# A hybrid decoder step: a quarter of the cached key pages split to fp16 rows in the even layer and transposed by DMA in the attention

## The chip, the cores and the metric

The kernel runs on one core of a Trainium2 chip. The metric is the device time of one launch in microseconds. Engine names are those of the profile: PE (TensorE matmuls), PEld (its weight loads), DVE (VectorE), ACT (ScalarE), POOL (GpSimd), SP (SyncE, whose queue issues most DMAs; its rows are named SPq).

## What is computed

One inference step of a decoder with two layers, for a prompt of 2048 tokens and for 8 sequences that each add 4 tokens to 2048 cached ones. The even layer has four heads of gated linear attention and four of "forgetting" attention, softmax attention with a bias from cumulated log forget gates; the odd layer is gated linear attention alone. The part that the change touches is the attention of the 8 sequences over their cached pages (a page is 128 tokens by 4 heads by 128 values, fp32; 16 pages a sequence, 128 in all, found through a page table):

```python
def fox_sample(q, k, v, log_f, k_pages, v_pages, logf_pages, page_table):
    k_past = k_pages[page_table].reshape(db, -1, H, dh)
    v_past = v_pages[page_table].reshape(db, -1, H, dh)
    ...
    logit_past = jnp.einsum('bthd,bshd->bhts', q, k_past).astype(jnp.float32) * scale \
        + cum_new[..., None] + suffix_past[:, :, None, :]
    ...
    p = jax.nn.softmax(jnp.concatenate([logit_past, logit_new], axis=-1), axis=-1).astype(v.dtype)
    return jnp.einsum('bhts,bshd->bthd', p[..., :P], v_past) + jnp.einsum('bhts,bshd->bthd', p[..., P:], v)
```

## The kernel before

Three phases follow each other on one core. `phase_even` computes the even layer's projections and its linear attention in two halves of 1024 tokens, `phase_fox` the forgetting attention of prompt and sequences, `phase_odd` both output projections, the odd layer and the final norm.

**Projections.** A product of fp32 values is made of three fp16 matmuls (`mm3`, L623 to L625: high times high, high times low, low times high). Weights are split into the two parts on the chip: ACT makes the high part (L353), DVE the low one (L354). A split needs a scale, a power of two, from the largest absolute value of the weights; for the weights of the output projections and of the odd layer it is measured early, beside the even layer's second half: `beside`, called from `staged`, runs `measure` (DVE's reductions at L300) and `scale` of the units in `later_units`. The names of their groups start with o (output projections), Cqk, Cv and Cg. A projection fills one of three PSUM banks (tag `pj`) and is copied out by ACT and DVE. The last unit is the attention's V (`Bv1`): DVE's copies and the low half at L1064 and L1071, ACT's high half at L1070, the stores to DRAM (`vd`) at L1085.

**Attention.** `fox_prompt` and `fox_sample` are generators; `until` draws from them in turn so that both advance by their shares FOX_P and FOX_S, and each `yield` tells what cost has been issued. A scheduler, which simulates the engines when the program is built, then puts the instructions of each engine in order; buffers are handed out by it when they come free. The prompt's blocks: scores (`s`, L623 to L625), bias and maximum on DVE (L1413), exponential with its sum on ACT (L1421), scaling on POOL (L1429), transposes on PE (L1449), split by ACT and DVE (L1456, L1457), and the product with V (`fo`). Its loads of q, k, v, bias and gate stand on SP's queue (L1375 to L1390), k by transposing DMA.

The sequences' keys go by 32 groups: 4 chunks of 512 tokens, in each the 8 sequences, for each 4 pages. A group's 4 pages are loaded by SP (L1543; the slots hold 25 pages). For each head, `turn` transposes its 4 pieces of 128 x 128 fp32 on PE into a PSUM bank (L1573, tag `kt`, two banks), and ACT (heads 0 and 2, L1577) or DVE (heads 1 and 3, L1578) copies them to one of eight key slots. Then `score` (L1632) multiplies the queries (32 columns for each head, zero but for this sequence's 4) with the 512 keys, as four fp32 strips side by side in the 32-column quarters of the array (`strips`). In the program a group's heads are turned before the group ahead of it is scored. After a chunk's 8 sequences, 16 small matmuls add the bias (L1661), and DVE takes the scores out with their running maximum (L1664). The values follow: 32 groups of 4 pages (L1711).

The sequences' queries (`qs`), keys, gates and values are loaded at L1555 and L1556, scaled by DVE (L1561), and spread to `qz` (L1565).

## Time and profile before

| | |
|---|---|
| median of 3 runs | 2329.38 us (2325.68 to 2329.55) |
| the profiled execution | 2327.94 us, span 2326.2 us |
| mean granted clock of TensorE | 0.991 |
| even layer's second half | about 480 to 856 us |
| attention, key pages | about 857 to 1077 us |
| attention, value pages | about 1077 to 1242 us |
| odd layer and output projections | from about 1272 us |

Times in the trace count from the span's start. A row of a timeline has the start, the length, the engine, line and operation, and in brackets the idle time of that engine just before and what ended it. The profiled execution is one more execution than the three of the median; it lies 0.06% below their median.

### The profile page before, as it was taken

To read this page: it belongs to the slowest core of one execution; us is meant where nothing else is said; L and a number is where in the kernel's file an instruction comes from. 1 tells how busy PE (TensorE), PEld (TensorE's weight loads), DVE (VectorE), ACT (ScalarE), POOL (GpSimd) and SP (SyncE) were. 2 spreads that over 40 slices of the span, in tenths; PEclk is the share of its full clock that TensorE was granted. 3 is DMA by queue.
4 is the path that set the end of the run, shared out by engine and by line. 5 is a ranking of instruction groups with operands and counts; after the bars stand their busy time and mean duration, and the time that the engine had idled before them with its cause. 6 is when DMAs were issued, how large, how long until landed. Compare 5 with 4: busy or idle time off the path is not lost.

```text
span 2326.2 us, 57896 instructions
## 1 busy us (share of the span) xinstructions
PE 2248.9 (97%) x23060; PEld 1604.3 (69%) x23060; DVE 1412.1 (61%) x3281; ACT 1018.5 (44%) x2264; POOL 733.7 (32%) x786
## 2 busy tenths in 40 slices
PE   7999999999999999999999999999999999999998
PEld 5667677855755875565446888677677666666887
DVE  7766568526654657667777445366675655557554
ACT  6434354211222225555566543545544544545343
POOL 2333334001201214223345345144552432322232
PEclk9999999999999999999999999999999999999999
DMA  7343444755432377875983969524234431115553
GB/s 238 120 128 105 146 127 164 201 142 160 143 120 73 125 189 251 245 242 196 276 262 102 335 195 263 132 79 137 74 102 96 121 96 58 49 56 164 176 181 150
DMA packets 357423, 361.64 MB, mean 155 GB/s; under 512 B 105777, under 2 KB 300658, under 8 KB 353058
## 3 DMA queue, kind: packets, MB, share of 16 engines
q1 hardware_dynamic: 355010, 351.33, 49.4%
q0 software_dynamic: 2144, 6.62, 0.8%
q8 instruction: 181, 2.97, 0.5%
q14 instruction: 88, 0.72, 0.1%
HBM read 244.54 MB, written 96.42 MB: 147 GB/s over the span
## 4 chain that ended last, share of the span: by engine, by line
PE 40%; DVE 5%; DMA 2%; ACT 2%; issue 1%; POOL 1%; SPq 1%; POOLq 0%; DVEq 0%; ACTq 0%
PE pt_o L623 4%; PE pt_o L624 4%; PE pt_o L625 4%; PE pt_Cv L623 2%; PE pt_Cv L624 2%; PE pt_Cv L625 2%; PE o_C L910 1%; PE gl_C L756 1%; PE pt L1449 1%; PE pv L1711 1%; DMA yr<-yT 1%; DMA wr_Cv<-in_w_in_odd 1%; PE py_C L728 1%; DVE scT L771 1%; PE fo L623 0%
## 5 line engine op out<-in xcount | busy, mean ns | idle before, releaser
L623 PE MATMUL pt_o<-w_o,act 128*128 128x256 f16 x1024 | 278.9, 273 | 1.9 <-ACT sg1C L680 1.9
L624 PE MATMUL pt_o<-w_o,act 128*128 128x256 f16 x1024 | 278.9, 273 | 0.0
L625 PE MATMUL pt_o<-w_o,act 128*128 128x256 f16 x1024 | 278.7, 273 | 0.0
L623 PEld LDWEIGHTS <-act 128*128 128x128 f16 x2304 | 226.1, 98 | 35.9 <-issue 3.6
L624 PEld LDWEIGHTS <-act 128*128 128x128 f16 x2304 | 226.2, 98 | 32.0 <-issue 3.4
L625 PEld LDWEIGHTS <-act 128*128 128x128 f16 x2304 | 226.2, 98 | 29.9 <-issue 1.7
L790 POOL TENSOR_TENSOR kA<-kA,fA 128x512 f32<-128x512 f32 (+1 forms) x56 | 80.9, 1445 | 344.8 <-PE gl_A L756 273.1
L623 PE MATMUL pt_Cv<-w_Cv,act 128*128 128x256 f16 (+1 forms) x512 | 141.3, 276 | 0.0
L624 PE MATMUL pt_Cv<-w_Cv,act 128*128 128x256 f16 (+1 forms) x512 | 141.3, 276 | 0.0
L625 PE MATMUL pt_Cv<-w_Cv,act 128*128 128x256 f16 (+1 forms) x512 | 141.2, 276 | 0.0
L790 POOL TENSOR_TENSOR kC<-kC,fC 128x512 f32<-128x512 f32 (+1 forms) x56 | 83.6, 1492 | 154.3 <-PE gl_C L756 103.1
L1429 POOL TENSOR_SCALAR L<-L,nm 128x512 f32<-128x512 f32 (+3 forms) x160 | 99.3, 635 | 103.5 <-DVE nm L1425 46.7
L1421 ACT ACTIVATE L<-L,nm,kc 128x512 f32<-128x512 f32 (+3 forms) x160 | 118.2, 740 | 27.5 <-DVE nm L1419 26.3
L1456 ACT ACTIVATE th<-pt 128x512 f16<-128x512 f32 (+3 forms) x159 | 81.8, 528 | 88.3 <-PE pt L1449 86.8
L1457 DVE TENSOR_TENSOR tl<-pt,th 128x512 f16<-128x512 f32 (+3 forms) x159 | 95.0, 609 | 20.7 <-ACT th L1456 18.9
L1449 PE MATMUL pt<-ident,L 128*128 128x128 f32 x544 | 91.4, 280 | 1.4 <-POOL L L1429 0.9
L1573 PEld LDWEIGHTS pkt<-ident,pgcache_fox_k 128*128 128x128 f32 x512 | 59.2, 142 | 44.2 <-issue 27.1
L1573 PE MATMUL pkt<-ident,pgcache_fox_k 128*128 128x128 f32 x512 | 78.5, 281 | 5.7 <-DVE kts L1578 1.7
L1449 PEld LDWEIGHTS pt<-ident,L 128*128 128x128 f32 x544 | 67.7, 144 | 23.3 <-DVE tl L1457 4.5
L1911 ACT ACTIVATE vC<-pt_Cv,kc 128x512 f32<-128x512 f32 (+1 forms) x40 | 23.9, 598 | 129.9 <-PE pt_Cv L625 129.9
L623 PE MATMUL pt_Bk<-w_Bk,act 128*128 128x256 f16 x256 | 70.2, 274 | 1.8 <-DVE Bvs L1071 1.8
L623 PE MATMUL pt_Av<-w_Ai,act 128*128 128x256 f16 x256 | 70.8, 277 | 0.5 <-ACT act L618 0.5
(959 smaller groups left out, 6566.6 us busy)
## 6 DMA issues: line engine op xcount, KB each, us to landing
pgcache_fox_k<-in_cache_fox_k SPq DMA_DIRECT2D x128, 256.0 KB, 4.2
pgcache_fox_v<-in_cache_fox_v SPq DMA_DIRECT2D x128, 256.0 KB, 4.2
yr<-yT SPq DMA_DIRECT2D x16, 1024.0 KB, 7.4
x1d<-xo SPq DMA_DIRECT2D x44, 256.0 KB, 4.7
wr_o<-in_w_out_even SPq DMA_DIRECT2D x32, 256.0 KB, 5.3
xo<-in_x_prompt SPq DMA_DIRECT2D x32, 256.0 KB, 5.5
wr_Cv<-in_w_in_odd SPq DMA_DIRECT2D x32, 256.0 KB, 3.9
x1r<-x1d SPq DMA_DIRECT2D x16, 512.0 KB, 4.9
```

Of the source, the lines that this page charges most:

```text
L623: nc.tensor.matmul(ps, lh[0], rh[0], start=first, stop=False)
L624: nc.tensor.matmul(ps, lh[0], rh[1], start=False, stop=False)
L625: return nc.tensor.matmul(ps, lh[1], rh[0], start=False, stop=last)
L728: nc.tensor.transpose(py[:, c * rows : (c + 1) * rows], on[:rows, c, t * P : (t + 1) * P], self.ident[:rows, :rows])
L790: nc.gpsimd.tensor_tensor(kv[:, :, 0], kv[:, :, 0], t1.to_broadcast([P, nb, w]), ALU.mult)
L1421: self.last_exp = nc.scalar.activation(lt[:, :w], lt[:, :w], AF.Exp, bias=nm[:, 0:1], scale=ib, accum_out=nm[:, 2 + j : 3 + j])
L1429: nc.gpsimd.tensor_scalar(lt[:, :w], lt[:, :w], nm[:, 1:2], 2.0**14, ALU.mult, ALU.mult)
L1449: nc.tensor.transpose(pt[:, w : w + P], rows[b][s // 4][0][:, (s % 4) * P : (s % 4 + 1) * P], self.ident)
L1456: nc.scalar.activation(th[:, a:w], pt[:, a:w], AF.Copy),
L1457: nc.vector.tensor_tensor(tl[:, a:w], pt[:, a:w], th[:, a:w], ALU.subtract)))
L1573: last = nc.tensor.transpose(pk[:, j * P : (j + 1) * P], pgs[j][:, h * P : (h + 1) * P], self.ident)
L1911: r = nc.scalar.activation(v[h][:, g : g + cnt], ps[:, :, :256], AF.Copy, scale=c)
```

## The change

Sequences 0 and 4 (`ROWED`), 32 of the 128 key pages, take another way.

In the even layer's second half, `page_rows` loads each of these pages, and for every row of a page (a token, all four heads) ACT adds up the absolute values, DVE bounds the sum from below and inverts it, ACT writes the scaled row as fp16 (the high part), DVE the remainder as fp16 (the low part), and SP stores 256 KB to DRAM (`kp`). `staged` draws from it at a pace (`PACE`): half a page at each step of 14 units and a whole one in the last. ACT's first step for a page also waits for the last projection matmul issued before it in the program. To make room on DVE, the measures named by `loose` (60 of those at L300) move to ACT, as sums of absolute values.

In the attention the 8 groups of these sequences come as two transposing DMAs of 512 KB each, straight into the layout that `score` needs: no transposes on PE, no copies. They are scored by 12 fp16 strips (`score3`: three products, four heads). As every row carries its own scale, `esc` brings the scales into the layout of the scores by 16 small matmuls a chunk, copied by ACT, and DVE's extraction multiplies by them instead of adding a zero; the bias is divided by the scales beforehand, and the other sequences' scales are 1. The queries are split to fp16 (`q16`, `qz16`).

Slots change: pages come in 6 slots of four, the turned keys have 4 slots instead of 8 (4 more, `pT`, serve the values' stage), the values' stage has 4 page slots of four. Group 0's two transposes and group 1's pages are asked for early, before the sequences' own loads.

```diff
+ROWED = (0, 4)
+SC_D = 10500.0
-S0 = 12000.0
+S0 = 6000.0
+SC_K = 1000.0
-FOX_S = 411000.0
+FOX_S = 500000.0
-PV_C = 5860.0
+PV_C = 5800.0
+PACE = [0] * 17 + [6] * 14 + [12]
...
+    def most(self, key, dst, x):
+        nc = self.nc
+        if not self.loose(key):
+            nc.vector.tensor_reduce(dst, x, mybir.AxisListType.XY, ALU.max, apply_absolute_value=True)
+            return
+        k, n = x.shape[1:]
+        nc.scalar.activation(self.junk()[:, : k * n].rearrange("p (k n) -> p k n", k=k), x, AF.Abs, scale=2.0**-10,
+                             accum_out=dst)
...
+        done = []
+        load(0)
+        for n in range(total):
+            load(n + 1)
+            m, s = self.km[:, n : n + 1], cols[n % 2]
+            x = fly.pop(n).rearrange("p (h d) -> p h d", h=NH)
+            t = pool.tile([P, NH, 2, P], F16, tag="pgs", name=f"kps{n}")
+            first = nc.scalar.activation(t[:, :, 0], x, AF.Abs, scale=2.0**-15, accum_out=m)
+            self.tc.add_manual_dep(first.ins, self.last_mm.ins.name, mybir.DependencyInfo(
+                mybir.DependencyClass.Sync, mybir.DependencyReason.DATA), reason="pages at the projections' pace")
+            nc.vector.tensor_scalar(m, m, TINY, None, ALU.max)
+            nc.vector.reciprocal(s, m)
+            nc.scalar.activation(t[:, :, 0], x, AF.Copy, scale=s)
+            nc.vector.scalar_tensor_tensor(t[:, :, 1], x, s, t[:, :, 0], ALU.mult, ALU.subtract)
+            if done:
+                store(*done.pop())
+            done.append((n, t))
+            yield
...
-                fs = Pool(s0, {"pg": PG, "kt": 8})
+                fs = Pool(s0, {"kt": 4, "pT": 4})
...
+        def page_cols(c, b):
...
+                for x in range(2):
+                    d = nc.sync.dma_start_transpose(
+                        t[:, 2 * x : 2 * x + 2].rearrange("p h x t -> p (h x) t"),
+                        self.kp[r : r + 512, x * 512 : (x + 1) * 512])
...
+            nc.vector.tensor_copy(q16[:, 0], qs)
+            nc.vector.tensor_tensor(q16[:, 1], qs, q16[:, 0], ALU.subtract)
+            for x in range(2):
+                for h in range(NH):
+                    nc.vector.tensor_tensor(qz16[:, x, h], q16[:, x, h : h + 1].to_broadcast([P, len(ROWED), TS]),
+                                            self.bmask[:, ROWED[0] :: ROWED[1] - ROWED[0]], ALU.mult)
...
+            if b in ROWED:
+                self.strips([score3(h, b, kt[0], sc, x, y) for x, y in ((0, 0), (0, 1), (1, 0)) for h in range(NH)],
+                            [kt[1]])
...
+                        nc.tensor.matmul(pe[32 * h : 32 * h + 32, j * P : (j + 1) * P],
+                                         env["sel"][:, 4 * c + j].rearrange("p b t -> p (b t)"), env["esc"][:, h],
+                                         start=True, stop=True, tile_position=(0, 32 * h))
+                et = fs.tile([P, 512], F32, tag="kt", name=f"escs{c}")
+                nc.scalar.activation(et, pe, AF.Copy)
```

How the instructions stand. The first place is SP's queue where the attention starts. Before, the last two loads of the prompt's second group, two stores of V (`vd`), the sequences' own loads, the last store of V, and the prompt's third group:

```order
L1386 DMA v_01_10717<-vd_74 128x4x256
L1390 DMA fsg_10722<-sgd 128x512
L1085 DMA vd_75<-Bvs_10537 128x2x512
L1085 DMA vd_75<-Bvs_10596 128x2x512
L1555 DMA qs<-qs 128x4x32
L1555 DMA kn<-ks 128x4x32
L1555 DMA sgs<-sgd 128x4x32
L1556 DMA vn<-vs 32x512
L1085 DMA vd_75<-Bvs_10655 128x2x512
L1382 DMA q_02_10793<-qd 128x2x512
```

Now, the same place up to the first page load (`kT` is a group of key pages as transposed by DMA; the last store of V is the one between the two):

```order
L1461 DMA_TRANSPOSE k_01_11419<-kd_72 128x2x512
L1452 DMA cb_11342<-cbd 128x512
L1617 DMA_TRANSPOSE kT_11356<-kp 128x4x512
L1108 DMA vd_75<-Bvs_11301 128x2x512
L1617 DMA_TRANSPOSE kT_11356<-kp 128x4x512
L1643 ISA
L1643 DMA pgcache_fox_k_11408<-in_cache_fox_k 128x512
```

and, after three more page loads like the last row, up to the sequences' first load:

```order
L1463 DMA v_01_11420<-vd_74 128x4x256
L1467 DMA fsg_11425<-sgd 128x512
L1459 DMA q_02_11496<-qd 128x2x512
L1461 DMA_TRANSPOSE k_02_11497<-kd_73 128x2x512
L1452 DMA cb_11342<-cbd 128x512
L1463 DMA v_02_11498<-vd_75 128x4x256
L1467 DMA fsg_11503<-sgd 128x512
L1672 DMA qs<-qs 128x4x32
```

The load of `qs` stood ahead of the last store of V; it now stands behind it, behind the second transpose, four page loads and two sets of the prompt's loads.

The second place is DVE at the same point, where the loaded queries are first read (`L` are the prompt's biased scores, `tl` low parts of its probabilities, `kts` turned keys). Before:

```order
L1457 TENSOR_TENSOR tl_10823<-pt_10819,th_10822 128x256
L1457 TENSOR_TENSOR tl_10856<-pt_10853,th_10855 128x128
L1419 TENSOR_SCALAR nm_10878<-mx_10864,kc 128x1
L1413 ISA L_10896,mx_10891<-s_10892,cb_10696 128x512
L1413 ISA mx_10891 128x1
L1413 ISA L_10902,mx_10891<-s_10898,cb_10696,mx_10891 128x384
L1413 ISA mx_10891 128x1
L1578 COPY kts_10992<-pkt_10987 128x512
L1413 ISA L_10902,mx_10891<-s_10898,cm_10889,mx_10891 128x128
L1413 ISA mx_10891 128x1
L1561 TENSOR_SCALAR qs<-qs,kc 128x64 x2
```

Now:

```order
L1490 ISA L_11596,mx_11591<-s_11592,cb_11342 128x512
L1490 ISA mx_11591 128x1
L1534 TENSOR_TENSOR tl_11526<-pt_11522,th_11525 128x256
L1676 CAST q_11367<-qs 128x128
L1703 COPY kts_11674<-pkt_11669 128x512
L1677 TENSOR_TENSOR q_11367<-qs,q_11367 128x128
L1680 TENSOR_TENSOR qz_11536<-q_11367,bmask 128x64 x4
L1685 TENSOR_SCALAR kn<-kn,kc 128x64 x2
```

The first reader of `qs`, the cast, stands ahead of the first copy of turned keys and of the scores that follow; before, the first reader stood behind both.

The third place is PE within a chunk, where a group's turning meets the scoring of the group ahead of it. Before:

```order
L1573 MATMUL pkt_12148<-ident,pgcache_fox_k_12146 128x128
L1632 MATMUL sc_12219<-kts_12026,qz 32x512
L1632 MATMUL sc_12219<-kts_12045,qz 32x512
L1632 MATMUL sc_12219<-kts_12052,qz 32x512
L1632 MATMUL sc_12219<-kts_12068,qz 32x512
L1573 MATMUL pkt_12162<-ident,pgcache_fox_k_12140 128x128
```

Now:

```order
L1698 MATMUL pkt_13263<-ident,pgcache_fox_k_13258 128x128 x4
L1769 MATMUL sc_12774<-kts_13157,qz 32x512
L1769 MATMUL sc_12774<-kts_13181,qz 32x512
L1769 MATMUL sc_12774<-kts_13188,qz 32x512
L1769 MATMUL sc_12774<-kts_13207,qz 32x512
L1698 MATMUL pkt_13282<-ident,pgcache_fox_k_13258 128x128 x4
L645 LDWEIGHTS v_03_11694
L645 MATMUL fo_13006<-th_13485,v_03_11694 128x128
```

The order is the same, the first head's transposes, the strips, the second head's transposes; but with four slots the copy of the first head's bank can only start behind the strips, and a prompt matmul follows ahead of the third head.

More of the change, by code (lines that the diff above doesn't have):

```diff
@@ L624, in mm3 @@
         nc.tensor.matmul(ps, lh[0], rh[1], start=False, stop=False)
-        return nc.tensor.matmul(ps, lh[1], rh[0], start=False, stop=last)
+        self.last_mm = nc.tensor.matmul(ps, lh[1], rh[0], start=False, stop=last)
+        return self.last_mm
     def proj_fm(self, pps, act, W, off, M, hf, evac, nm):
@@ L1141, in phase_even @@
             us, lins = [], []
+            self.pages = self.page_rows(wp)
+            self.paged = 0
+            self.junk = lambda: nrm.tile([P, D], BF16, tag="th", name="junk")
             def beside(x):
@@ L1290, in staged @@
                     beside(2 * j + n // 2)
+                if beside and j > 2:
+                    self.paged += PACE[j]
+                    while self.paged >= 12:
+                        self.paged -= 12
+                        next(self.pages, None)
                 yield c
@@ L1545, in page, with fetch @@
             return t, d
+        def fetch(n):
+            c, b = n // DB, n % DB
+            if b in ROWED:
+                return page_cols(c, b)
+            return [page("cache_fox_k", b, 4 * c + j)[0] for j in range(4)]
+        held, ahead = {}, {0: fetch(0)}
+        for nm, shape in (("vn", [TS, 512]), ("sgs", [P, NH, TS]), ("ys", [P, NH, DB, DS]), ("pTn", [TS, DB, NH, DS]),
+                          ("qs", [P, NH, TS]), ("kn", [P, NH, TS]), ("stri", [P, P]), ("mpg", [P, DB, NPG])):
+            held[nm] = one(shape, nm)
+        q16 = fs.tile([P, 512], F32, tag="kt", name="q16").bitcast(F16)[:, : 2 * NH * TS].rearrange(
+            "p (x h t) -> p x h t", x=2, h=NH)
+        held["pr"] = one([P, T + TS], "pr")
+        order[1:3] = [1, 2]
+        x1 = pg("hold")
+        held["qz"] = one([P, NH, DB, TS], "qz")
+        ahead[1] = fetch(1)
         yield S0
@@ L1639, in fox_sample @@
                 c, b = n // DB, n % DB
-                pgs = [page("cache_fox_k", b, 4 * c + j)[0] for j in range(4)]
-                new = []
-                for h in range(NH):
+                got = ahead.pop(n) if n in ahead else fetch(n)
+                if b in ROWED:
+                    kts.append(got)
                     steps.append(self.last_pe)
-                    with self.tc.issue_after(steps[max(0, len(steps) - KAHEAD)].ins):
-                        new.append(turn(c, b, h, pgs))
-                    yield SC_C
-                kts.append(new)
+                    yield SC_D
+                else:
+                    new = []
+                    for h in range(NH):
+                        steps.append(self.last_pe)
+                        with self.tc.issue_after(steps[max(0, len(steps) - KAHEAD)].ins):
+                            new.append(turn(c, b, h, got))
+                        yield SC_K
+                    kts.append(new)
             if n == PAST // NH:
```

117 lines of the change are left out of this document (92 added, 25 removed).

## The prediction

> **What bounds the kernel now.** I read the page first, then the engines' busy time by stage, then the groups of the attention and PE's timeline, and last the queues around the point where the attention starts. The page's first part:
>
> ```profile
> PE 2248.9 (97%) x23060; PEld 1604.3 (69%) x23060; DVE 1412.1 (61%) x3281; ACT 1018.5 (44%) x2264; POOL 733.7 (32%) x786
> ```
>
> TensorE is busy for 97% of the span, so time falls only where its work falls or its waits go. The stages that the change touches, in a table of stretches (length, then busy time of PE, PEld, DVE, ACT and POOL with counts, the granted clock, the busy share of the DMA engines, GB/s): the even layer's second half, the attention while it scores key pages, the attention over value pages, and its tail.
>
> ```profile
> 480.00:856.00 376.00, 372.52 (x3961) 241.01 (x3959) 204.37 (x506) 80.19 (x211) 53.01 (x49) 1.00 0.42 129
> 857.00:1077.00 220.00, 210.05 (x1527) 131.18 (x1528) 150.97 (x457) 122.59 (x278) 68.81 (x132) 0.96 0.78 240
> 1077.00:1242.00 165.00, 157.10 (x1043) 80.37 (x1042) 120.71 (x405) 98.22 (x233) 64.31 (x115) 1.00 0.76 239
> ```
>
> In the key stage PE is busy for 210 of 220 us, DVE for 69% and ACT for 56%: the stage is PE's, with 10 us of waits. In the even layer's half PE waits for 3.5 us of 376, while DVE stands at 54% and ACT at 21%. So the change takes work from the engine that bounds the key stage and puts other work on engines that have room in a stage that PE bounds as well. Its groups in the attention (line, engine, operation, count, then busy time and mean ns of one, then idle time ahead of them and what ended it):
>
> ```profile
> L1573 PE MATMUL pkt<-ident,pgcache_fox_k 128*128 128x128 f32 x512 | 78.5, 281 | 5.7 <-DVE kts L1578 1.7 <-DMA pgcache_fox_k<-in_cache_fox_k 1.6 <-ACT kts L1577 1.4
> L1573 PEld LDWEIGHTS pkt<-ident,pgcache_fox_k 128*128 128x128 f32 x512 | 59.2, 142 | 44.2 <-issue 27.1 <-DVE kts L1578 3.8 <-ACT kts L1577 2.7
> L1578 DVE COPY kts<-pkt 128x512 f32<-128x512 f32 x64 | 44.0, 688 | 28.8 <-PE pkt L1573 28.6
> L1577 ACT ACTIVATE kts<-pkt 128x512 f32<-128x512 f32 x64 | 38.0, 593 | 57.1 <-PE pkt L1573 57.0
> L1661 PE MATMUL sc<-suf,sel 128*32 128x128 f32 x128 | 5.1, 277 | 0.0
> ```
>
> The mean of one matmul (281 ns) counts overlap with its neighbours; the busy time divided by the count does not, and that is the price I use.
>
> **Part by part: the attention.** Turning: 128 of the 512 transposes go. At 78.5/512 = 0.153 us each that is 19.6 us; by the weight loads alone (59.2/512 = 0.116 us) it is 14.8. Matmul ends are modelled and overlap, so I take the middle, 0.135 us: **−17.2 us**. Their 16 DVE copies (16 x 0.688 = 11.0 us) and 16 ACT copies (9.5 us) go too, but neither engine bounds the stage: nothing by themselves. The idle time ahead of L1573 is 5.7 us; a quarter of it goes with a quarter of the groups, and I count **−1.0**, since part of it is the first pages' arrival.
>
> Scoring: 8 of the 32 groups change from 4 fp32 strips to 12 fp16 strips. On PE's timeline (start, length, instruction, count):
>
> ```profile
> 964.64 1.06 PE L1632 MATMUL sc<-kts,qz 128*32 128x512 f32 x8
> 965.64 0.55 PE L1573 MATMUL pkt<-ident,pgcache_fox_k 128*128 128x128 f32 x3
> ...
> 864.72 0.38 PE L623 MATMUL s<-k,q 128*128 128x512 f16 x1 [0.25 <-DVE mx L1413]
> 864.94 0.38 PE L624 MATMUL s<-k,q 128*128 128x512 f16 x1
> ```
>
> A group of four fp32 strips lasts 1.00 us from start to start. An fp16 matmul over 512 columns follows the one before after 0.22 us. The fp32 strips run side by side (a group of four in 1.00 us); no row shows fp16 strips doing so. If they do, 12 strips are three rounds, 0.65 us, and 8 groups save 8 x 0.35 = 2.8; if they don't, a group lasts 12 x 0.22 = 2.6 us and 8 cost 12.8 more. I take **−2.8**, because they are placed like the fp32 ones. The 64 matmuls for the scales have the shape and number of those at L1661: **+5.1**. One more transpose and the 4 copies on ACT hold the single score bank a little longer at each chunk's end: **+0.6**, bounded by four ACT copies at 0.593 (2.4).
>
> Slots: the turned keys have 4 slots where they had 8, so the copy of a group's first head now waits for the strips of the group before. Behind that copy, on ACT, stand the exponentials of the prompt's softmax; on PE, the group's third head waits for the copy to free its bank. After the strips PE has the second head's transposes (4 x 0.135 = 0.54 us) against a copy of 0.593: 0.05 us a group if ACT is free, 0.85 if an exponential of 0.8 us stands ahead of it:
>
> ```profile
> L1421 ACT ACTIVATE L<-L,nm,kc 128x512 f32<-128x512 f32 x112 | 90.1, 805 | 24.6 <-DVE nm L1419 23.4 <-POOL L L1429 0.3
> ```
>
> For 24 groups that is 1 to 20 us. In the new order prompt matmuls stand between the second and third head in most groups, so I take **+2**.
>
> Transfers: 32 page loads become 16 transposes of 512 KB. Transposes of that size run back to back once in this trace (the queue's row, then that stretch; the key pages' loads from the page's part 6):
>
> ```profile
> 1785.13 19.15 SPq L592 DMA_TRANSPOSE act<-xs  x8
> 1785.00:1804.50 19.50, 19.50 (x272) 14.67 (x270) 9.57 (x26) 6.08 (x12) 1.54 (x1) 1.00 1.06 204
> pgcache_fox_k<-in_cache_fox_k SPq DMA_DIRECT2D x128, 256.0 KB, 4.2
> ```
>
> That is 2.4 us each and 204/1.06 = 192 GB/s at a full share, against 240/0.78 = 308 for the key stage. 8.4 MB then take 44 us of DMA time for 27: the share goes from 0.78 to 0.86. Still under full, and the slots hold 24 pages where they held 25, so I count nothing; pages that came late would show as waits of L1573 on DMA, now 1.6 us.
>
> **Part by part: the attention's start.** Here the queues change. Rows of DVE, of SP's queue and of PE, and two stretches of 20 us:
>
> ```profile
> 856.44 0.48 DVE L1071 SCALAR_TENSOR_TENSOR Bvs<-pt_Bv,kc,Bvs 128x256 f16<-128x256 f32 x1 [0.47 <-ACT Bvs L1070]
> 869.06 0.60 DVE L1457 TENSOR_TENSOR tl<-pt,th 128x256 f16<-128x256 f32 x2
> 871.95 0.67 DVE L1561 TENSOR_SCALAR qs<-qs,kc 128x64 f32<-128x64 f32 x2
> 851.71 0.50 SPq L1555 DMA_DIRECT2D qs<-qs  x1
> 856.95 0.36 SPq L1085 DMA_DIRECT2D vd<-Bvs  x1
> 861.18 2.44 SPq L1543 DMA_DIRECT2D pgcache_fox_k<-in_cache_fox_k  x4
> DMA to landing us min/median/max: 4.3/4.3/4.3
> 857.02 0.27 PE L623 MATMUL s<-k,q 128*128 128x128 f16 x1 [3.43 <-DMA vn<-vs]
> 840.00:860.00 20.00, 16.57 (x137) 13.22 (x135) 9.48 (x26) 4.36 (x11) 4.24 (x8) 0.89 1.00 257
> 860.00:880.00 20.00, 17.25 (x93) 9.52 (x91) 16.47 (x68) 10.89 (x28) 8.62 (x17) 0.84 1.10 306
> ```
>
> Before, the load of `qs` was issued at 851.7, ahead of the last store of V (856.95), and landed after 4.3 us (the row on landing is that of this load); DVE first read it at 871.95. In the new order that load stands behind the last V store, a second 512 KB transpose (2.4 us), four page loads (2.44) and two sets of the prompt's loads, about ten short issues of 0.5 us: 857.3 + 2.4 + 2.4 + 5 = 867, landed at 871. DVE's first reader, the cast to fp16, has moved forward, to where the trace has L1457's `tl` of 256 columns, 868.5 to 869.6. So DVE would stand there for 2 to 3 us with key copies and the prompt's maxima behind it, and PE waits on both. On the other side the first pages are now asked for some 6 us ahead, which may take away the 1.6 us of waits on them. I take **+3**, from 0 to 10.
>
> The upper end is with the clock. The 3.43-us wait before 857.02 (the profile names a DMA; what ended last is DVE's row at 856.44) stands ahead of a granted clock of 0.89 and 0.84: another such wait would cost 0.11 x 20 + 0.16 x 20 = 5 us more. The Trainium skill, "TensorE: Matmul & The Clock Gate", Part 1, says that the clock is either half or full and falls to half after an idle window of about 3.4 us; the two rows agree with that as far as they go, and by it a stall of 2 to 3 us would cost its own length only. The Trainium skill's "DMA: Bandwidth & Descriptors", Latency and other measured facts, has 261 GB/s for a transposing DMA, so 2.0 us for one of 512 KB, against the 2.4 measured here; by that figure, as an estimate, the stall is 0.4 us shorter.
>
> **Part by part: the even layer's half.** Its prices (a weight measure and a division on DVE, the same split done on weights by DVE and ACT, reading an accumulator on ACT), and the longest waits of PE in that half:
>
> ```profile
> L300 DVE TENSOR_REDUCE rm_o<-lr_o 128x1 f32<-128x512 f32 x24 | 14.8, 676 | 0.0
> L280 DVE RECIPROCAL kc<-kc 128x1 f32<-128x1 f32 x23 | 3.7, 159 | 0.4
> L354 DVE SCALAR_TENSOR_TENSOR w_Bk<-wr_Bk,kc,w_Bk 128x512 f16<-128x512 f32 x2 | 2.1, 1046 | 0.0
> L353 ACT ACTIVATE w_Bk<-wr_Bk,kc 128x512 f16<-128x512 f32 x2 | 1.4, 704 | 0.0
> L719 ACT ACTIVATION_READ_ACCUMULATOR on_A<-o_A 128x1 f32 x40 | 8.4, 210 | 0.0
> PE pf_Bg L623 <- ACT Bg L680: 0.5, 1, 0.5
> 848.39 0.75 DVE L1064 TENSOR_SCALAR Bv<-pt_Bv,kc 128x512 f32<-128x512 f32 x1 [2.35 <-PE pt_Bv L625]
> 853.63 0.75 DVE L1064 TENSOR_SCALAR Bv<-pt_Bv,kc 128x512 f32<-128x512 f32 x1 [2.35 <-PE pt_Bv L625]
> ```
>
> DVE loses 60 measures (60 x 0.676 = 40.6 us) and gains for 32 pages 1.05 + 2 x 0.16 each (43.8): even. ACT gains 60 x (0.70 + 0.21) + 32 x (0.70 + 0.21 + 0.70) = 106 us; put wholly on this half's 80 busy us that is 186 of 376, still half free. A page holds ACT for some 2 us in one stretch (two passes with DVE's divisor between), behind which stand the projections' copies. A bank of a projection fills in 5.24 us (848.39 to 853.63) and there are three: two stand between a late copy and a waiting PE. I take **+1.5**, from 0 to 16 (half a microsecond a page). Loads and stores of 2 x 8.4 MB in a half at a DMA share of 0.42 cost nothing by the same cover.
>
> **The sum.** −17.2 − 1.0 − 2.8 + 5.1 + 0.6 + 2 + 3 + 1.5 = −8.8 us against the profiled execution's 2327.94 us (span 2326.2), or −0.4%. The median of the three runs is 2329.38, so 2320.6 for the median. A measurement of this kernel can tell about 0.2% from no change, 4.7 us: below 2324.7 is faster, above 2334.0 slower.
>
> **The rivals.**
> More (14%): the turns' waits and the first pages' wait go entirely and the transposes are worth their busy time, −19.6 − 1.4 − 1.6 − 2.8 + 5.1 = −20.3, **2309**. For it: PEld's 44 us of idle time at L1573, so a transpose may take its slot longer than its weights. Against: it needs the start and the even half for nothing.
> The slots eat it (14%): four slots for turned keys make ACT's copy wait for the strips in every group, at 0.6 us a group 14.4 instead of 2: 2320.6 + 12 = **2333** at most, about **2329** with half the groups exposed; no change. For it: ACT's copies stand in one queue with 112 exponentials of 0.8 us. Against: ACT has 44% of the stage free, and prompt matmuls between the heads cover it.
> The start (9%): DVE's stall at the cast is over 3.4 us and the half clock is paid again: 4.6 + 5 instead of 3, **2327**, no change. It decides from the moment `qs` lands after 872.
> The even half holds PE (15%; the side of slower): ACT waits for a projection's last matmul ahead of each page, then through DVE's divisor, and the copies of the following bank come late. At 0.5 us a page 16 instead of 1.5, **2335**; it is slower by over 0.2% from 0.47 us a page on (13.4 more than in the sum). For it: ACT's and DVE's steps of a page wait for each other in turn, on queues that run in order. Against: the three banks and PE's 3.5 us of waits now.
> That the change does not do what it says can be left out: 384 transposes for 512 stand in the new order.
>
> **How the numbers follow.** The forecast has 48%, with a range of its own from 2315 to 2326. Faster: 42 of these, the 14 of the first rival, and 3 of the others: 0.59. No change within 0.2%: 6 + 11 + 7 + 1 = 0.25. Slower: 0.16, nearly all of it the even half. The range from 2308 to 2335 leaves out half of the first rival and the even half's upper end, and holds fp16 strips that do not run side by side (+15.6, 2336) but for a microsecond.
>
> **What would show it.** Right: the turns (L1698 in the changed kernel) with 384 matmuls and some 59 us of busy time; the scores at rowed groups in 0.65 us; in the even half no wait of PE over a microsecond and ACT at half; at the start a DVE wait on the load of `qs` of 2 to 3 us. Wrong: waits of the turns on ACT's copies of several us in sum; strips that follow each other at 0.22; PE waits on the even layer's copies; a granted clock under 0.84 after 860; pages that come late.

## The result, and the profile after

The changed kernel takes 2342.43 us in the median of 9 runs (2340.55 to 2346.91), the kernel before 2329.38 in 9 runs beside it (2324.56 to 2338.47). The ratio is 1.0061, 95% interval 1.0050 to 1.0073: slower by 0.6%, outside the forecast range (2308 to 2335) and on the other side of no change. The profiled execution took 2342.38 us, its span is 2340.6.

The first line of the page after, and then the table of its stages (the even layer's half, the key stage, the values' stage; columns as before):

```profile
PE 2243.3 (96%) x23093; PEld 1599.3 (68%) x23093; DVE 1399.0 (60%) x3312; ACT 1094.0 (47%) x2472; POOL 733.5 (31%) x792
```
```profile
480.00:856.00 376.00, 372.72 (x3957) 240.61 (x3954) 203.28 (x546) 155.64 (x409) 51.33 (x46) 1.00 0.52 166
859.00:1100.50 241.50, 226.62 (x1770) 143.11 (x1771) 175.67 (x566) 141.68 (x333) 89.39 (x169) 0.97 0.85 223
1100.50:1246.00 145.50, 126.24 (x817) 59.20 (x815) 86.87 (x288) 70.49 (x167) 46.44 (x83) 0.96 0.83 263
```

TensorE's work did fall, by 5.6 us in the span. The time was lost in waits of TensorE, 20 us more than before, and in the clock behind them: the values' stage ran at 0.96 where it ran at 1.00, the first 24 us of the output projections at 0.93 instead of 1.00. The first matmul of each stage says where (us in the two traces):

| from, to | before | after | |
|---|---|---|---|
| start, attention | 857.0 | 859.1 | +2.1 |
| attention, first value matmul | 232.0 | 255.0 | +23.0 |
| first to last value matmul | 151.4 | 131.6 | −19.8 |
| tail of the attention | 35.9 | 38.8 | +2.9 |
| output projections, to the odd layer | 171.7 | 179.1 | +7.4 |
| the rest, to the last projection matmul | 869.4 | 868.3 | −1.1 |

The first row tells nothing: among the traces with an unchanged even layer the attention starts anywhere from 857.0 to 859.6 us. The key stage is longer because the change gave it a larger share of the prompt's work; the attention as a whole is 6.1 us longer where 10 less were forecast, and the output projections, whose matmuls the change does not touch, are 7.4 longer. The groups of the attention and PE's longest waits (us, times, longest), with the wait on value pages before as the last row:

```profile
L1698 PE MATMUL pkt<-ident,pgcache_fox_k 128*128 128x128 f32 x384 | 59.7, 283 | 7.6 <-DVE kts L1703 4.3 <-DMA pgcache_fox_k<-in_cache_fox_k 2.6 <-ACT kts L1702 0.4
L1871 PE MATMUL pv<-pgcache_fox_v,pT 128*16 128x512 f32 x256 | 33.9, 610 | 18.7 <-DMA pgcache_fox_v<-in_cache_fox_v 17.0 <-DVE sel L1880 1.7
L1817 PE MATMUL esc<-esc,sel 128*32 128x128 f32 x128 | 4.7, 276 | 0.2 <-ACT kts L1702 0.2
```
```profile
PE pv L1871 <- DMA pgcache_fox_v<-in_cache_fox_v: 17.0, 17, 4.0
PE pkt L1698 <- DVE kts L1703: 4.3, 3, 2.9
PE pt_o L645 <- ACT w_o L382: 4.0, 1, 4.0
```
```profile
PE pv L1711 <- DMA pgcache_fox_v<-in_cache_fox_v: 2.6, 3, 1.1
```

The turns shrank from 78.5 to 59.7 us as forecast. But PE now waits 17.0 us for value pages (2.6 before), and 4.0 at the first weights of the output projections. A wait "for a DMA" has three possible causes: the transfer is slow, its slot comes free late, or its queue asks for it late. The three were told apart on the chip.

### The profile page after: what moved, and what is told of

It reads as the page before. It is cut to its first block, busy times and chain, and to the rows that moved or that the text cites. A ratio compares the mean times of both kernels' runs of the same rounds, so it can differ in the third digit from the quotient of the medians.

```text
span 2340.6 us, 58207 instructions
## 1 busy us (share of the span) xinstructions
PE 2243.3 (96%) x23093; PEld 1599.3 (68%) x23093; DVE 1399.0 (60%) x3312; ACT 1094.0 (47%) x2472; POOL 733.5 (31%) x792
## 4 chain that ended last, share of the span: by engine, by line
PE 78%; DVE 7%; DMA 5%; issue 3%; POOL 2%; ACT 2%; SPq 2%; POOLq 0%; DVEq 0%; ACTq 0%
PE pt_o L645 4%; PE pt_o L646 4%; PE pt_o L647 4%; PE pt_Cv L645 2%; PE pt_Cv L646 2%; PE pt_Cv L647 2%; PE pkt L1698 2%; PE pt L1526 2%; DMA pgcache_fox_v<-in_cache_fox_v 2%; PE pt_Bv L645 1%; PE pt_Bv L646 1%; PE pt_Bv L647 1%; PE pf_Ag L647 1%; PE pf_Ag L645 1%; PE pf_Ag L646 1%
## 5 line engine op out<-in xcount | busy, mean ns | idle before, releaser
L645 PE MATMUL pt_Av<-w_Ai,act 128*128 128x256 f16 x256 | 71.0, 277 | 0.5 <-ACT act L640 0.5
L646 PE MATMUL pt_Av<-w_Ai,act 128*128 128x256 f16 x256 | 70.8, 276 | 0.4 <-DVE w_Ai L376 0.4
L647 PE MATMUL pt_Bk<-w_Bk,act 128*128 128x256 f16 x256 | 71.0, 277 | 0.0
L645 PE MATMUL pt_Bk<-w_Bk,act 128*128 128x256 f16 x256 | 71.0, 277 | 0.0
```

The source lines that it names most:

```text
L645: nc.tensor.matmul(ps, lh[0], rh[0], start=first, stop=False)
L646: nc.tensor.matmul(ps, lh[0], rh[1], start=False, stop=False)
L647: self.last_mm = nc.tensor.matmul(ps, lh[1], rh[0], start=False, stop=last)
```

## The experiments

Times are medians in us, ratios are to the kernel before as run beside each, with their 95% interval; the kernel before gave 2327 to 2332 there.

### Transfers, slots or stage length

Run e1, six page slots of four in the values' stage instead of four:

```diff
-        order[:] = [0, 3, 4, 5]
+        order[:] = [0, 3, 4, 5, 1, 2]
```

> The changed kernel, with all six slots of four pages in the values' stage where it has four. Theory of the slots: PE's 17.0 us of waits on value pages come from having 16 page slots there instead of 25; with 24 they fall under 5 us, and the time falls by 10 or more, to 2332 or less. Theory of the stage's length: the values' stage is shorter (145.5 us instead of 164, since the key stage took a larger share of the prompt), the same 33.5 MB of pages run at 0.83 of the DMA engines, and slots do not matter: waits stay at 12 us or more, time within 3 us of 2342. A third outcome: the two slots' memory is wanted by the output projection's first weights, and what the values gain is paid there: pages' waits fall, the time stays within 4 us.

Measured 2342.18, ratio 1.0060 (1.0037 to 1.0082). The values' stage:

```profile
1112.00:1242.00 130.00, 113.34 (x730) 52.26 (x729) 76.33 (x251) 60.88 (x147) 42.36 (x74) 0.95 0.86 268
```

and PE's wait on value pages:

```profile
PE pv L1871 <- DMA pgcache_fox_v<-in_cache_fox_v: 14.2, 8, 3.6
```

The waits stay. Slots alone are not the cause. Then the bytes, in the changed kernel (e7) and in the kernel before (e8): only the first half of each value page is loaded, and the matmuls read it twice, so that TensorE's work is as it was; half of the values are left out.

```diff
+                m = 256 if cache == "cache_fox_v" else 512
-                d = nc.sync.dma_start(t, i[cache][0, bass.ds(reg, 1)].rearrange("o s h d -> (o s) (h d)"))
+                d = nc.sync.dma_start(t[:, :m], i[cache][0, bass.ds(reg, 1)].rearrange("o s h d -> (o s) (h d)")[:, :m])
...
+                        rhs = rhs[:, :256].unsqueeze(1).to_broadcast([P, 2, 256])
```

> The changed kernel, with half of the bytes of each value page loaded (256 of 512 columns; the matmuls read them twice, so that TensorE has the same work; half of the values are left out). Theory of the transfers: the values' stage runs at what the DMA engines give, 260 GB/s at a shown share of 0.82, and a page lands only just in time (issue to use 4.4 us, a landing takes 3.9). With 17 MB less, PE's 17.0 us of waits on value pages fall under 4 us and the time falls by 10 to 18, to between 2324 and 2332. Theory of the slots: a page is asked for only when a slot of four comes free, whatever its size: waits stay at 8 us or more, time 2337 or more.

> The kernel before, with the same halving of the value pages' bytes (half of the values left out, TensorE's work unchanged). If the attention before was TensorE's alone, as the prediction has it, nothing is gained: within 3 us of the kernel before. If the transfers were already close to their limit there (share 0.81 in the values' stage), it gains 4 us or more.

Measured 2345.74 (1.0069, 1.0050 to 1.0089) for the changed kernel, 2328.03 (0.9989, 0.9974 to 1.0005) for the kernel before. The values' stage of the changed kernel with half the bytes, PE's wait, and the landing of the value pages, first in the changed kernel as it was, then with half the bytes:

```profile
1113.00:1245.00 132.00, 113.64 (x734) 51.33 (x732) 77.18 (x254) 61.52 (x145) 42.35 (x74) 0.96 0.55 161
```
```profile
PE pv L1873 <- DMA pgcache_fox_v<-in_cache_fox_v: 16.2, 13, 3.3
```
```profile
DMA to landing us min/median/max: 2.5/3.9/6.7
```
```profile
DMA to landing us min/median/max: 1.9/2.2/4.6
```

The DMA engines went from 0.82 to 0.55 of their time and a page lands in 2.2 us instead of 3.9, and the stage is 132 us long as ever, with 16.2 us of waits. It is not the transfers: the theory that I held by then fell with this run. Nor does the kernel before gain from it. What remains is that the pages are asked for late.

Three runs on the stage's length: the prompt's shares of before in the changed kernel (e6), 16 page slots in the kernel before (e5, where `pg` hands out tags pg0 to pg24 in turn), and in the changed kernel e1's slots, e6's shares and the order of e3, below, together (e9):

```diff
-SC_D = 10500.0
+SC_D = 3344.0
-SC_K = 1000.0
+SC_K = 836.0
-FOX_S = 500000.0
+FOX_S = 407000.0
```
```diff
+        slot[0], n_slot[0] = 0, 16
         pT = [fs.tile([P, 512], F32, tag="kt", name=f"pT{g}")
```

> The changed kernel, with the shares of the prompt as they were before: the key stage's steps cost 3344 for a rowed group and 4 x 836 for others (10500 and 4 x 1000 in the change) and FOX_S is 407000, so that the key stage has 30% of the prompt instead of 39% and the values' stage 48% instead of 39%. Theory of the stage's length: the values' stage is about 160 us long again, PE's waits on value pages fall from 17 to under 7 us, and the time to about 2331. Theory of the slots: 16 slots starve it at any length, waits of 10 us or more stay. Rival: the key stage, now some 25 us shorter with the same transposing DMAs, takes the waits instead: waits of the key stage's turns and strips on DMA rise by 10 us, time within 4 us of 2342.

> The kernel before, with 16 page slots in the values' stage instead of 25 (25 as before in the key stage), each handed out singly. Theory of the slots: PE's waits on value pages rise from 2.6 us to 10 or more, time 2337 to 2345. Theory of the stage's length: at 164 us the pages come in time with 16 slots as well: waits under 6 us, time 2329 to 2333.

> The changed kernel with three things undone together: six page slots in the values' stage (as in e1), the order of the first weights' load (as in e3), and the prompt's shares of before (as in e6). If slots cost what they cost the kernel before (17 us from 25 to 16) once the stage has its old length, 2346 - 7 - 17 = 2322. If they are worth what they were worth in e1 (nothing in the time), 2346 - 7 = 2339. In between, 2330, if the longer stage needs slots and the key stage still pays for the transposes.

Measured 2346.14 (1.0077, 1.0043 to 1.0110), 2344.33 (1.0072, 1.0048 to 1.0096) and 2342.72 (1.0050, 1.0031 to 1.0069). The values' stage took 160, 170 and 157 us, PE's waits on value pages 13.7, 12.8 and 9.0. So a longer stage alone does not cure it, and 16 slots cost the kernel before 17 us. In that one, SP stands for 21.3 us, up to 1071, at a load of the prompt, whose slot PE has yet to free, with value pages behind it; the first of them is asked for at 1074.0, where it was at 1039.4, and the stage starts at 1089.7:

```profile
SPq L1384 <- PE pt L1449: 21.3, 1, 21.3
```

That the 17 us come from there is argued, not shown; but it turned me to SP's queue.

### SP's queue

In the changed kernel's values' stage SP hardly waits for anything: its waits there are 3.4 us at the longest and 7.8 in all. Page loads follow each other with hardly a pause (SP's timeline: start, length, count), and these are its instructions in the stage (ns, least, median and most; first and last start), the last row the table loads of three groups with nothing between them:

```profile
1115.18 31.60 SPq L1643 DMA_DIRECT2D pgcache_fox_v<-in_cache_fox_v  x32
1149.46 25.43 SPq L1643 DMA_DIRECT2D pgcache_fox_v<-in_cache_fox_v  x25
```
```profile
L1634 SPq FUSED_REGOPS  x104: 147/152/161, 1121.7 to 1237.5; - x104
L1634 SPq SEQ_ASSERT  x104: 18/18/18, 1121.9 to 1237.7; - x104
L1634 SPq TENSOR_LOAD <-scTs x26: 862/871/1882, 1120.8 to 1235.8; - x26
```
```profile
L1643 SPq DMA_DIRECT2D pgcache_fox_v<-in_cache_fox_v x112: 332/333/1184, 1115.2 to 1239.5; - x112
```
```profile
L1634 SPq TENSOR_LOAD <-scTs x3: 871/872/885, 1134.5 to 1142.7; - x3
```

For every four pages SP loads four indices from the page table (0.87 us), checks each (4 x 0.17 us) and issues four loads (4 x 0.33 us and two small register steps). With the gaps between these instructions a group takes (1142.7 − 1134.5)/2 = 4.1 us, and with the prompt's loads between them a group comes every (1235.8 − 1120.8)/25 = 4.6 us. 28 groups are asked for after the first sixteen pages: 129 us. The stage is 131.6 us long, and 129.5 to 131.9 in the four other runs that kept the change's shares and the checks (e1, e7, and e3 and e10 below): SP's work, with few waits, fills it. None of it counts as busy on a page of the profile.

Of the runs on the stage's length, e6 fits this in part: 9.7 of its 13.7 us of waits lie ahead of 1160, where SP again issues 32 pages in a row and PE uses a page 4 to 9 us after it was asked for; later ones are asked for up to 17 us ahead.

```profile
1095.58 29.97 SPq L1643 DMA_DIRECT2D pgcache_fox_v<-in_cache_fox_v  x32
```

With the slots undone as well (e9), 9.0 us of waits stay; what makes those pages late is not shown.

The checks are 1 us of a group, with what lies between them (4.1 us with them, 3.1 without, below), and can be left out, in the changed kernel (e11) and in the kernel before (e12):

```diff
-                        vals, (mybir.EngineType.SP,), min_val=0, max_val=n_pool - 1)
+                        vals, (mybir.EngineType.SP,), min_val=0, max_val=n_pool - 1,
+                        skip_runtime_bounds_check_because="the page table holds indices of the pool")
```

> The changed kernel, without the bounds checks of page indices on SP (for each four pages eight register instructions out of one table load, eight checks and four page loads; nothing else of the computation changes). Theory of SP's queue: in the values' stage SP spends 4.05 us for each group of four pages without waiting for anything, 32 x 4.05 = 130 us, and that is the stage's length in the changed kernel and in e1, e3, e7 and e10 (129.5 to 131.9 us), whatever the bytes and slots are. The checks are 1.0 us of the 4.05, so the stage falls to what PE needs, about 115 to 120 us, PE's waits on value pages to 5 us or less, the time by 10 to 15, to about 2329. Theory of the transfers or of the slots: SP is not the limit, the time stays within 3 us of 2342.

> The kernel before, without the same checks. SP spends as much there for each group, but the values' stage is 151 us long, 25 pages are there when it starts, and SP waits for slots in between: by the theory of SP's queue at most 2 us are gained. If the gain is 5 us or more, SP bound the kernel before as well.

Measured 2326.46, ratio 0.9978 (0.9966 to 0.9990) for the changed kernel, 2333.38, ratio 1.0017 (1.0004 to 1.0029) for the kernel before. The changed kernel without the checks: its values' stage, PE's wait on value pages, SP's page loads, and two table loads within these, one group apart:

```profile
1114.00:1229.00 115.00, 109.20 (x736) 49.99 (x735) 77.25 (x256) 61.31 (x147) 42.10 (x74) 1.00 0.94 312
```
```profile
PE pv L1872 <- DMA pgcache_fox_v<-in_cache_fox_v: 3.2, 3, 1.2
```
```profile
1115.91 22.71 SPq L1644 DMA_DIRECT2D pgcache_fox_v<-in_cache_fox_v  x28
```
```profile
L1634 SPq TENSOR_LOAD <-scTs x2: 872/876/881, 1122.5 to 1125.5; - x2
```

28 pages now take 22.7 us of SP's queue, a group some 3.1 (1122.5 to 1125.5), the stage is 113 us long, PE's waits are 3.2 us, the clock is back at 1.00, and the DMA engines, which e7's first theory held to be at their limit at 260 GB/s, move 312. The time fell by 0.8% from this one edit; the same edit gives the kernel before nothing. The other way round, the kernel before with its value groups' indices loaded and checked twice (f4):

```diff
+                    for _ in range(2 if cache == "cache_fox_v" else 1):
+                        _, regs[:] = nc.values_load_multi_w_load_instructions(
-                    _, regs[:] = nc.values_load_multi_w_load_instructions(
```

> The kernel before, with the table load and the checks of each value group done twice on SP (nothing else changed). SP's work for a group is then 4.05 + 1.9 = 6 us; 26 of 32 groups are asked for after the first seven, and 26 x 6 = 156 us against a stage of 151: by the theory of SP's queue the values' stage becomes SP's, 165 us or longer, PE's waits on value pages rise from 2.6 to 10 or more, the time to 2340 or more. If transfers or slots set the pace, nothing changes: within 3 us of the kernel before.

PE's wait on value pages, and the table loads on SP, in that stage:

```profile
PE pv L1712 <- DMA pgcache_fox_v<-in_cache_fox_v: 30.2, 8, 7.0
```
```profile
L1537 SPq TENSOR_LOAD <-scTs x46: 859/865/1234, 1096.9 to 1258.2; - x46
```

Measured 2372.05, ratio 1.0166 (1.0147 to 1.0185). 23 groups in 161 us are 7 us each where 6 were expected, the stage 193 us for 165 or more. SP's queue binds that kernel too as soon as it is made dearer: before, SP's waits among the page and prompt loads of the stage came to some 24 us, and the run adds 23 x 1.9 = 44 us of work. The Trainium skill, "DMA: Bandwidth & Descriptors", section "Issuing engines are not separate DMA queues", says that spreading DMAs over issuing engines saves only the time on the sequencer, which is usually small beside the DMA. Here it is not: a page costs 4.1/4 = 1.03 us of queue in the changed kernel, and its 256 KB would take 0.84 us at the 312 GB/s of the row above, an estimate.

### The first weights' load

On SP's queue at the end of the attention, before the change and after it (wr_o are weights, yr the attention's results):

```profile
1229.65 1.93 SPq L335 DMA_DIRECT2D wr_o<-in_w_out_even  x4
1231.75 41.24 SPq L1801 DMA_DIRECT2D yr<-yT  x3
1273.40 2.30 SPq L335 DMA_DIRECT2D wr_o<-in_w_out_even  x4
```

and in the changed kernel:

```profile
1239.97 1.94 SPq L357 DMA_DIRECT2D wr_o<-in_w_out_even  x4
1242.08 45.99 SPq L1961 DMA_DIRECT2D yr<-yT  x5
1288.12 2.97 SPq L357 DMA_DIRECT2D wr_o<-in_w_out_even  x4
```

Five loads of results stand ahead of the second weights where three stood; they wait for the attention's end, and the weights with them. In run e3 the two that are too many were put behind (`first_wr` is the last load of those weights):

```diff
+            with tc.issue_after(first_wr.ins):
+                pieces = load(self.y_pieces(1, 0, act, wpool))
-            pieces = load(self.y_pieces(1, 0, act, wpool))
```

> The changed kernel, with the two loads of the second half's attention output put behind the second weights' load on SP's queue, as they stood before the change. Theory of the order: those loads wait for the attention's last results and hold the weights back, which shows as PE's waits of 4.0 and 1.0 us on the weights' split at the start of the output projections and as a clock of 0.93 behind them; without that the stretch from the first output projection matmul to the first of the odd layer is 172 us again instead of 179, and the time 2335. Rival: the weights are late anyway, since their slot or the attention's end is late: 2340 or more.

Measured 2335.48, ratio 1.0034 (1.0021 to 1.0047), with the stretch at 171.7 us:

```profile
1239.60 34.95 SPq L1961 DMA_DIRECT2D yr<-yT  x3
1274.64 2.44 SPq L357 DMA_DIRECT2D wr_o<-in_w_out_even  x4
```

As expected. Both edits together, e3's and e11's (e13):

> The changed kernel without the checks and with the order of the first weights' load (e3) put right. The two losses lie in different stages, so they should add: 2342 - 7 (e3) - 12 (e11, if the theory of SP's queue holds) = 2323, below the kernel before. If the clock or the waits move instead of going, 2330.

Measured 2318.08, ratio 0.9951 (0.9934 to 0.9969), 12 us below the kernel before; they add. Its key stage, its values' stage and its output projections:

```profile
859.00:1113.00 254.00, 237.83 (x1835) 149.08 (x1836) 184.46 (x593) 149.82 (x350) 94.41 (x181) 0.97 0.84 228
1116.00:1229.00 113.00, 107.94 (x731) 49.41 (x728) 76.75 (x253) 60.43 (x145) 42.10 (x74) 1.00 0.95 317
1267.40:1439.00 171.60, 171.60 (x1634) 151.74 (x1632) 84.09 (x100) 76.07 (x122) 81.17 (x57) 1.00 0.83 260
```

### The other terms

On top of e13, one thing each: the sequences' own loads asked for ahead of group 1's pages (e14), eight key slots (f1), and e1's six page slots (e15).

```diff
+        for t, d in ((held["qs"], self.qs), (held["kn"], self.ks), (held["sgs"], self.sgd[:, :, T : T + TS])):
+            nc.sync.dma_start(t, d.rearrange("h p t -> p h t"))
+        nc.sync.dma_start(held["vn"], self.vs)
         ahead[1] = fetch(1)
```
```diff
-                fs = Pool(s0, {"kt": 4, "pT": 4})
+                fs = Pool(s0, {"kt": 8})
```

> As e13, and the sequences' own loads asked for ahead of group 1's pages instead of behind them and the prompt's next loads. Theory of the start: DVE's stall at the cast, seen as PE's wait of 2.9 us on a key copy at 880 and as a busy time of PE of 14 us out of 21 after 859, goes or shrinks: 3 to 5 us below e13. Rival: the loads are held by the transposes ahead of them, or the first pages are late by as much: within 2 us of e13.

> As e13 (2318), with eight slots for turned keys as before the change, in place of four and four more for the values' stage. By the term of the sum (+2 for the four slots) the time falls by 1 to 3, to 2316; by the rival (0.6 us a group) by 10 or more, to 2308. Slots that the schedule already covers: within 1.5 us of 2318.

> As e13 (2318), with six page slots of four in the values' stage. With SP's queue free, PE's waits on value pages are 3.0 us in e13: at most 3 us to gain, 2315 to 2318. If more slots delay the first weights, whose memory they share: 2320 or more.

Measured 2317.74 (0.9950, 0.9930 to 0.9969), 2316.17 (0.9930, 0.9917 to 0.9943) and 2317.12 (0.9935, 0.9920 to 0.9950): none is clear of e13, whose interval overlaps all three; the ratios of f1 and e15 are 0.2% lower, by the medians 2 and 1 us. In e14 DVE waits for the queries for 3.8 us instead of 8.7, and the wait of PE at the start only moves, from a key copy to the first page and to the strips (PE's waits):

```profile
PE pkt L1699 <- DMA pgcache_fox_k<-in_cache_fox_k: 4.0, 1, 4.0
PE sc L1774 <- DVE qz L1681: 3.5, 1, 3.5
```

The even layer's part alone, put into the kernel before (f2: `most`, `loose`, `page_rows`, `PACE` and their calls, nothing of the attention), and the same with e3's edit (f5):

> The kernel before, with only the even layer's part of the change: the 32 pages split and stored (nobody reads them), the 60 measures on ACT. By the term of the sum +1.5, 2332; by the rival of the even half (half a microsecond a page) +16, 2346. The trace of the changed kernel has the attention start 2 us later than before, which speaks for the term.

> As f2 (the kernel before with the even layer's part alone, 2347), with the order of the first weights' load put right as in e3. If that order is what the even part costs beyond its own stage, 2347 - 7 = 2340, and what is left of the 15 us lies in the attention, whose loads stand in another order on SP's queue there. If all of it was the order: 2333.

Measured 2346.91 (1.0072, 1.0055 to 1.0088) and 2341.03 (1.0048, 1.0034 to 1.0062). The attention starts at 858.4 and 857.9 us in them, within the 857.0 to 859.6 of the traces with an unchanged even layer, so the half itself costs too little to be told. But 6 us are the order of the weights' load, which comes with this part of the change, 400 us ahead of where it is paid: the output projections take 177.8 us in f2 and 171.8 in f5. The other 10 lie in the attention, 11 us longer in the trace of f5 with no wait over 5; what in its order does that stays open, and so does whether the changed kernel pays it too.

Plain loads in place of the transposing ones, in the changed kernel (e10); the keys of sequences 0 and 4 then stand untransposed, so that this kernel leaves out their scores:

```diff
-                    d = nc.sync.dma_start_transpose(
+                    d = nc.sync.dma_start(
...
-                        self.kp[r : r + 512, x * 512 : (x + 1) * 512])
+                        self.kp[r + 256 * x : r + 256 * x + 256].rearrange("(a p) c -> p a c", p=P))
```

> The changed kernel, with plain loads of the same 512 KB from the same buffer in place of the 16 transposing DMAs (the keys of sequences 0 and 4 are then not transposed, so their scores are left out of what is computed rightly). Theory: a transposing DMA runs at 192 GB/s for 308 of a plain one and holds SP's queue for 3.3 us at the median; without it the key stage loses 17 us of DMA time and some 30 us of SP's queue, the DVE wait at the attention's start (PE 2.9 us) shrinks, and the time falls by 3 to 8. Rival: the transposes are hidden as forecast: within 2 us of 2342.

Measured 2351.74 (1.0097, 1.0073 to 1.0120), slower. It does not isolate the price of the transposes: at the attention's start PE now waits 8.7 us for the queries, and the key stage is 263 us long for 255.

## Why the prediction was wrong

**The step that failed** is the one on transfers: "Still under full, and the slots hold 24 pages where they held 25, so I count nothing". It asked whether the DMA engines had room, in the key stage, and there it held: the turns' waits on pages are 2.6 us, 1.6 before. The limit was the queue that asks for the pages, in the values' stage, for which the sum has no term at all; the 24 slots are the key stage's, and the values' stage has 16. The change shortens that stage, since it removes TensorE's work from the key stage and moves the prompt's work there to fill it, and 16 pages are asked for ahead of it where 25 were. The 128 value pages cost SP's queue as much as ever, and SP now sets the stage's pace: PE waits 17.0 us for pages, 2.6 before. The edit that takes 1 us a group off SP gave 16 us. That rival was not in the list: a stage without removed work, made shorter, in which another queue ends last. How much the shorter stage and how much the smaller head start did is not separated: undoing either alone leaves 14 us of waits (e6, e1), undoing both 9.0 (e9).

**The second loss**, 6 to 8 us, has no term in the prediction either. I compared the order of instructions at the attention and on PE behind it, not on SP's queue at the odd layer's start, where the schedule had put two waiting loads ahead of one that PE needs.

**What held.** Without these two losses the change gains 12 us (7 to 15 by the interval), against the sum's 8.8 and its 2320.6. That the two lie so close is in part luck: e13 also leaves out the checks, which are worth nothing in the kernel before (e12), the start cost more than its term, and f2's 10 us in the attention stay unexplained. The terms: the turns 59.7 us of PE for 384 (59 forecast). A group of twelve fp16 strips takes 0.77 us, so they do run side by side, for 0.65 forecast:

```profile
1004.38 0.83 PE L1773 MATMUL sc<-kT,qz 128*32 128x512 f16 x12
1005.15 1.09 PE L1698 MATMUL pkt<-ident,pgcache_fox_k 128*128 128x128 f32 x8
```

The scales' matmuls 4.7 us (5.1). The even layer's half: too little to be told (1.5), with ACT at 156 us of 376 (186 at most was forecast); PE's waits on the even layer's copies, the rival on the slower side, did not come. The key slots: 2 us by f1's median, not clear of the noise (2).

The start was dearer than forecast. The queries' load was issued at 874.7, not 867: the first transpose holds the queue for 4.42 us ahead of the last store of V, which was through at 864.0 instead of 857.3, and a transposing load of the prompt took 2.61 where 0.5 was counted. DVE stood at the cast for 9.3 us, where 2 to 3 were forecast, and PE is busy for 29 of the attention's first 40 us, where it was for 37 (the last two rows, before and after):

```profile
858.93 4.42 SPq L1617 DMA_TRANSPOSE kT<-kp  x1
874.71 0.42 SPq L1672 DMA_DIRECT2D qs<-qs  x1
```
```profile
879.72 0.23 DVE L1676 CAST q<-qs 128x128 f16<-128x128 f32 x1 [9.33 <-DMA qs<-qs]
```
```profile
880.60 1.97 PE L1698 MATMUL pkt<-ident,pgcache_fox_k 128*128 128x128 f32 x8 [2.91 <-DVE kts L1703]
```
```profile
857.00:897.00 40.00, 37.23 (x208) 21.26 (x209) 30.79 (x117) 23.95 (x59) 22.82 (x52) 0.85 1.00 295
859.00:899.00 40.00, 29.05 (x135) 14.30 (x135) 23.07 (x99) 16.20 (x40) 17.01 (x40) 0.83 1.10 253
```

That is 8 us more idle time for a term of 3, and the condition of the rival on the start came true. Its price did not: asking for the queries earlier gained nothing (e14). The granted clock falls, recovers and falls again here in both kernels; its mean over the 40 us is 0.85 before and 0.83 after, so the clock cost hardly more. Its first fall now stands behind a wait of 3.0 us (0.66 from 859 to 864), so the prediction's reading that a stall of 2 to 3 us costs its own length only is not safe.

The 24 us between the changed kernel and its repaired form are the two causes above, 16 and 8 by the medians, 19 and 6 by the ratios.

## What to carry to other kernels

When work is taken from the engine that bounds a stage, ask of every queue how long it needs for that stage, and of the stages beside it that the schedule will stretch or shrink; a queue that only issues is on no list of busy engines, and "waits for a DMA" can mean a DMA that was asked for late. Halving the bytes and leaving the issue alone tells the two apart in one run. And where a scheduler orders the queues, compare the order at places that the change does not touch, too.

## What was not expected of the hardware

Four page indices read into SP's registers take 0.87 us, a check of one 0.17, the issue of a load 0.33: with register steps and gaps 4.1 us of queue for 1 MB, so that this path asked for no more than about 256 GB/s of pages, while the DMA engines move 312 to 317 GB/s, the prompt's loads among them, in the same stage once the checks are gone. A shown DMA share of 0.82 was therefore no sign of a limit, as 0.95 in the repaired kernel shows.
